# Memory attention of two token tiles written step by step in turn, in a transformer block on one core

## The chip, the cores and the metric

The kernel runs on one core of a Trainium2 chip. The core has five engines with a queue of instructions each, and every queue is worked off in order: TensorE (PE, matrix products and transposes, with its weight loads listed as PEld), VectorE (DVE), ScalarE (ACT), GpSimd (POOL) and SyncE (SP, which here only issues transfers). Matrix products land in PSUM, everything else lives in SBUF, and data comes from HBM by DMA. The metric is the device time of one execution in microseconds (us); lower is better.

## What is computed

One transformer block over 1024 tokens of width 1024, in float32: a mixer of two sparse attentions, then an attention over 256 memory rows, then a squared-ReLU MLP of width 4096. Only the middle one is touched:

```python
def _memory_xattn(h, mem, mem_norm_g, w_xq, w_xk, w_xv, xq_norm_g, xk_norm_g, w_xo):
    m = _rms_norm(mem, mem_norm_g)
    q = _rms_norm((h @ w_xq).reshape(B, L, 4, 128), xq_norm_g)
    k = _rms_norm((m @ w_xk).reshape(B, M, 4, 128), xk_norm_g)
    v = (m @ w_xv).reshape(B, M, 4, 128)
    s = jnp.einsum('bqhd,bmhd->bhqm', q, k) * (128 ** -0.5)
    p = jax.nn.softmax(s, axis=-1)
    o = jnp.einsum('bhqm,bmhd->bqhd', p, v).reshape(B, L, 512)
    return o @ w_xo

x = x + _hybrid_mixer(_rms_norm(x, norm1_g), ...)
x = x + _memory_xattn(_rms_norm(x, norm2_g), mem, ...)
x = x + _sq_relu_mlp(_rms_norm(x, norm3_g), w_ff_in, w_ff_out)
```

## The kernel before

The 1024 tokens are eight tiles of 128 rows. The work falls into two kinds. The mixer's attention (`attend`, tiles 0 to 7, eight units of output per tile, each ended by the addition at L716) has many small steps that pass from PE to DVE, ACT and POOL and back. The "fill" is the rest: projections of the second half of the tokens, the memory's keys and values (`memory`), then for tiles 0-1 and 2-3 what lies between the mixer and the MLP (`between`), the MLP of tiles 0 to 3 (`mlp`), and `between` of tiles 4-5. `together` takes turns between the two by paces written in the kernel. When the attention is done, what is left of the fill runs beside `between` of tiles 6-7 (`merge`), and the MLP of tiles 4 to 7 ends the kernel.

`between` handles two tiles: it reads the mixer's output and x, multiplies by `w_out` (L218 through `gemm`, four chunks of 256 columns; `add_to`, L899, adds the result to the residual), normalizes each tile (`norm_T2`: square and sum at L293, scale at L297, eight transposes at L274, copies out of PSUM), multiplies by `w_xq` in two chunks of 256 columns (two heads each), does the memory attention of each tile and chunk, writes the result to HBM (`xo`, L972) and reads it back (L978), transposes it, multiplies by `w_xo`, and adds it to the residual. `mlp` then normalizes its four tiles in the same way, but with the copies split in a high and a low part (ACT at L235, DVE at L236).

One item of memory attention, for one tile and one chunk, is `consume_q`, called by `gemm` as soon as the product with `w_xq` stands in PSUM. Its steps:

1. square (ACT, L934), sum (DVE, L936), gain (DVE, L937), root (DVE L229, POOL L231) and two scales (DVE L940, L941);
2. two transposes (PE, L274) and the split of the result (ACT L235, DVE L236);
3. six score products (PE), row maximum (DVE, L950, L951), two exponentials (ACT, L954);
4. four transposes (PE, L959) and their split;
5. twelve products with the values (PE), division (DVE, L971) and the write of `xo` (SP, L972).

The products with `w_out`, `w_xq` and `w_xo` are plain float32: PE takes each as two passes, two records of the trace.

PSUM is handed out in rings. In `between` of tiles 0 to 5 the ring `D` (two buffers) holds the product with `w_xq`, the scores and the products with the values, in this order; the ring `M` (one buffer) holds the transposes. Tiles 6-7 use `S` (two) and `PT` (two) instead. The SBUF ring `h` has eight buffers; keys and values of a chunk take four of them (loaded on POOL's queue at the first tile of a chunk), an item takes three.

The order in which the lines are written is not yet the order on the engines. At build a scheduler lays the instructions out for each engine, by written order and by when it reckons each one's inputs and buffers to be ready. The order that it arrives at is then fixed.

Of the kernel before, what the change touches and what calls it, by code (L numbers as in the profile page):

```python
# [166 lines left out]
def build(nc, tc, I, C, out):  # L167
# [13 lines left out]
    def pst(tag, shape):  # L181
        return psum["pool"].tile(shape, F32, tag=tag, name="ps" + tag, bufs=psum["n"][tag],
                                 padded_shape=[P, 512 // int(np.prod(shape[2:]))] + list(shape[2:]))

    def ring(pool, tag, shape, dt=F32):
        n = RINGS[pool.name if isinstance(pool.name, str) else "dn"][tag]
        return pool.tile(shape, dt, tag=tag, name=tag, bufs=n)
# [46 lines left out]
    def split_ps(src, hi, lo):  # L234
        s.activation(hi, src, AF.Copy)  # L235
        v.tensor_tensor(lo, src, hi, op=ALU.subtract)  # L236
# [31 lines left out]
    def to_T(pool, x_t, xs, nk):  # L268

        for c in range(0, nk, 4):  # L270
            m = min(4, nk - c)
            pt = pst(TAGS[pool.name][1], [P, m, P])
            for j in range(m):
                te.transpose(pt[:, j, :], x_t[:, (c + j) * P:(c + j + 1) * P], ident)  # L274
            if len(xs) == 2:
                split_ps(pt, xs[0][:, c:c + m, :], xs[1][:, c:c + m, :])
            elif c % 8 == 0:
                s.activation(xs[0][:, c:c + m, :], pt, AF.Copy)
            else:
                v.tensor_copy(xs[0][:, c:c + m, :], pt)  # L280
# [19 lines left out]
    def gemm(pool, xs, nk, nt, wsrc, chunks, consume):  # L300

        for ci, parts in enumerate(chunks):
            w = sum(n for _, n in parts)
            gr = []
            for k0 in range(0, nk, KG):
                kn = min(KG, nk - k0)
                srcs, o = [], 0
                for c0, n in parts:
                    srcs.append((lambda r, o=o, n=n: r[:, :, o:o + n],
                                 wsrc[k0 * P:(k0 + kn) * P, c0:c0 + n].rearrange("(k p) n -> p k n", p=P)))  # L310
                    o += n
                ws = load_w(pool, [P, kn, w], *srcs) if len(xs) == 2 else load_whole(pool, [P, kn, w], *srcs)
                gr += [[x[:, k, :] for x in ws] for k in range(kn)]
            for t in range(nt):
                pt = pst(TAGS[pool.name][0], [P, w])
                for k in range(nk):
                    if len(xs) == 1:
                        mm(pt, xs[0](t, k), gr[k][0], k == 0, k == nk - 1)
                        continue
                    wh, wl = gr[k]  # L320
                    xh, xl = xs[0](t, k), xs[1](t, k)
                    mm(pt, xh, wh, k == 0, False)
                    mm(pt, xh, wl, False, False)
                    mm(pt, xl, wh, False, k == nk - 1)
                consume(ci, t, pt)
                yield nk * (5 - len(xs)) * w / 2400.0
# [13 lines left out]
    def gain2(pool, src):  # L340
        gs = [ring(pool, "h", [P, 512]) for _ in range(2)]
        for i, gb in enumerate(gs):
            nc.sync.dma_start(gb, row(src[i * 512:(i + 1) * 512]).to_broadcast([P, 512]))
        return gs
# [550 lines left out]
    def residual_add(x2):  # L895
        def add_to(ci, t, pt):
            w = pt.shape[-1]
            dst = x2[t][:, ci * w:(ci + 1) * w]
            v.tensor_tensor(dst, pt, dst, op=ALU.add)  # L899
        return add_to  # L900

    def between(pool, t0, nt, x2s, keep):

        o_of = []
        for t in range(nt):
            o = ring(pool, "b4", [P, 8, P])
            for c in range(8):
                nc.sync.dma_start(o[:, c, :], oT_dr[t0 + t][c])
            o_of.append(o)
        x2 = [ring(pool, "b4", [P, DM]) for t in range(nt)]  # L910
        for t in range(nt):
            nc.sync.dma_start(x2[t], I["x"][0, (t0 + t) * P:(t0 + t + 1) * P, :])
        add_to = residual_add(x2)
        four = [[(c * 256, 256)] for c in range(4)]
        yield from gemm(pool, [lambda t, k: o_of[t][:, k, :]], 8, nt, W["w_out"], four, add_to)
        _, xf, xt_of = xT(pool, nt, True)

        gb2 = gain2(pool, W["norm2_g"])
        for t in range(nt):
            norm_T2(pool, x2[t], gb2, xt_of(t))  # L920
            yield 1.0

        kx = []

        def consume_q(ci, t, pt):
            if t == 0:
                kx[:] = [[ring(pool, "h", [P, 2, 256], F32R) for _ in range(2)] for _ in range(2)]
                for a in range(2):
                    g.dma_start(kx[0][a], KX[a][ci])
                    g.dma_start(kx[1][a], VX[a][ci])  # L930
            (kh, kl), (vh, vl) = kx
            q = ring(pool, "relu", [P, 2, 2, P])
            p3 = pt.rearrange("p (h d) -> p h d", d=P)
            s.activation(q[:, 1], p3, AF.Square)  # L934
            ss = small(pool, "xss", 2)
            v.tensor_reduce(ss, q[:, 1], axis=AX.X, op=ALU.add)  # L936
            v.tensor_tensor(q[:, 0], p3, xqg[:, None, :].to_broadcast([P, 2, P]), op=ALU.mult)  # L937
            r = rsqrt_of(pool, ss, P, 2, "xq")
            sc = small(pool, "xsc", 4).rearrange("p (a h) -> p a h", a=2)
            v.tensor_scalar(sc[:, 0, :], r, XSCALE, None, op0=ALU.mult)  # L940
            v.tensor_scalar(sc[:, 1, :], r, -XSCALE, None, op0=ALU.mult)  # L941
            qhl = ring(pool, "h", [P, 2, 2, P], F32R)
            to_T(pool, q[:, 0].rearrange("p h d -> p (h d)"), [qhl[:, 0], qhl[:, 1]], 2)
            sp = pst(TAGS[pool.name][0], [P, 2, 256])
            for h in range(2):
                mm(sp[:, h, :], qhl[:, 0, h, :], kh[:, h, :], True, False)
                mm(sp[:, h, :], qhl[:, 0, h, :], kl[:, h, :], False, False)
                mm(sp[:, h, :], qhl[:, 1, h, :], kh[:, h, :], False, True)
            nb, sums = small(pool, "xnb", 2), small(pool, "xsum", 2)
            v.tensor_reduce(nb, sp, axis=AX.X, op=ALU.max)  # L950
            v.tensor_tensor(nb, nb, sc[:, 1, :], op=ALU.mult)  # L951
            pr = ring(pool, "relu", [P, 2, 256])
            for h in range(2):
                s.activation(pr[:, h, :], sp[:, h, :], AF.Exp, bias=nb[:, h:h + 1],  # L954
                             scale=sc[:, 0, h:h + 1], accum_out=sums[:, h:h + 1])
            p2 = pst(TAGS[pool.name][1], [P, 2, 2, P])
            for k in range(2):
                for h in range(2):
                    te.transpose(p2[:, k, h, :], pr[:, h, k * P:(k + 1) * P], ident)  # L959
            ph, pl = ring(pool, "h", [P, 2, 2, P], F32R), ring(pool, "h", [P, 2, 2, P], F32R)  # L960
            split_ps(p2, ph, pl)
            pv = pst(TAGS[pool.name][0], [P, 2, P])
            for h in range(2):
                hs = slice(h * P, (h + 1) * P)
                for k in range(2):
                    mm(pv[:, h, :], ph[:, k, h, :], vh[:, k, hs], k == 0, False)
                    mm(pv[:, h, :], ph[:, k, h, :], vl[:, k, hs], False, False)
                    mm(pv[:, h, :], pl[:, k, h, :], vh[:, k, hs], False, k == 1)
            v.reciprocal(sums, sums)
            o = ring(pool, "relu", [P, 2, P])  # L970
            v.tensor_tensor(o, pv, sums[:, :, None].to_broadcast([P, 2, P]), op=ALU.mult)  # L971
            nc.sync.dma_start(xo_dr[t0 + t][:, ci * 256:(ci + 1) * 256], o.rearrange("p h d -> p (h d)"))  # L972

        yield from gemm(pool, xf, 8, nt, W["w_xq"], [[(0, 256)], [(256, 256)]], consume_q)

        for t in range(nt):
            o = ring(pool, "relu", [P, 512])
            nc.sync.dma_start(o, xo_dr[t0 + t])  # L978
            to_T(pool, o, [x[:, 0:4] for x in xt_of(t)], 4)
            yield 0.5  # L980
        yield from gemm(pool, xf, 4, nt, W["w_xo"], four, add_to)
        for t in range(nt):
            if keep:
                x2s[t0 + t] = x2[t]
            else:
                nc.sync.dma_start(x2_dr[t0 + t], x2[t])
# [151 lines left out]
```

## Time and profile before

| | us |
|---|---|
| median of 3 runs | 1861.02 |
| lowest, highest | 1859.41, 1865.53 |
| the profiled execution | 1861.12 |
| span of its trace, first to last instruction | 1859.0 |

| engine | busy us | share of the span |
|---|---|---|
| PE | 1729.4 | 93% |
| ACT | 1077.2 | 58% |
| DVE | 934.9 | 50% |
| POOL | 894.7 | 48% |

The memory attention's items start (L934) at 485.7, 500.4, 521.1 and 545.3 us for tiles 0-1, at 620.7, 636.9, 656.8 and 677.3 us for tiles 2-3, and between 1364.9 and 1439.8 us for tiles 4 to 7, where two `between` run side by side. The first eight lie beside the mixer's attention. In rows of the timeline a matmul's line begins with its start in us and its duration; `x4` counts records that follow each other; `[1.84 <-DMA whi]` is idle time before it and who ended it. A busy PE is not PE at its peak, so in what follows idle time is read together with the number of records in a stretch and with the granted clock.

### The profile page before, as it was taken

To read this page: it belongs to the slowest core of one execution; us is meant where nothing else is said; L and a number is where in the kernel's file an instruction comes from. 1 tells how busy PE (TensorE), PEld (TensorE's weight loads), DVE (VectorE), ACT (ScalarE), POOL (GpSimd) and SP (SyncE) were. 2 spreads that over 40 slices of the span, in tenths; PEclk is the share of its full clock that TensorE was granted. 3 is DMA by queue.
4 is the path that set the end of the run, shared out by engine and by line. 5 is a ranking of instruction groups with operands and counts; after the bars stand their busy time and mean duration, and the time that the engine had idled before them with its cause. 6 is when DMAs were issued, how large, how long until landed. Compare 5 with 4: busy or idle time off the path is not lost. (4 is left out here: it accounts for less than half of the span.)

```text
span 1859.0 us, 28028 instructions
## 1 busy us (share of the span) xinstructions
PE 1729.4 (93%) x9262; PEld 1467.8 (79%) x9262; DVE 934.9 (50%) x2353; ACT 1077.2 (58%) x2687; POOL 894.7 (48%) x1034
## 2 busy tenths in 40 slices
PE   5996999899989987899998999999898899999999
PEld 5995988678877776688886888888787778788787
DVE  4554766566773786466545565565333332222222
ACT  4444658898697678756984569975223233333332
POOL 2365557455451344466764766664111134444553
PEclk9998998999999998899999999999998999999999
DMA  8225413166226231121221221222773313222232
GB/s 198 71 86 163 98 35 99 65 212 178 90 86 193 88 83 42 46 70 56 77 77 57 67 72 60 64 71 93 241 249 109 116 63 97 91 91 91 91 98 101
DMA packets 180081, 187.50 MB, mean 101 GB/s; under 512 B 34657, under 2 KB 149089, under 8 KB 179937
## 3 DMA queue, kind: packets, MB, share of 16 engines
q1 hardware_dynamic: 172000, 175.23, 31.2%
q0 software_dynamic: 7936, 10.49, 2.1%
q8 instruction: 73, 1.20, 0.3%
q14 instruction: 72, 0.58, 0.1%
HBM read 164.69 MB, written 20.97 MB: 100 GB/s over the span
## 5 line engine op out<-in xcount | busy, mean ns | idle before, releaser
L249 POOL TENSOR_TENSOR wlo<-wraw,whi 128x512 fp32r<-128x512 f32 (+1 forms) x230 | 308.2, 1349 | 322.3 <-ACT whi L244 265.0
L244 ACT ACTIVATE whi<-wraw 128x512 fp32r<-128x512 f32 (+2 forms) x289 | 180.9, 628 | 251.8 <-PE psS L218 150.0
L218 PE MATMUL psD<-whi,xh 128*128 128x256 f32 (+1 forms) x704 | 192.7, 357 | 5.8 <-ACT whi L244 3.5
L218 PE MATMUL psD<-wlo,xh 128*128 128x256 f32 (+1 forms) x704 | 192.5, 354 | 0.8 <-DMA wlo<-in_w_in_dram 0.6
L218 PE MATMUL psD<-whi,h 128*128 128x512 f32 x512 | 177.1, 406 | 9.4 <-POOL h L1024 3.7
L236 DVE TENSOR_TENSOR pl<-psPT,ph 128x512 fp32r<-128x512 f32 (+1 forms) x232 | 141.8, 620 | 62.2 <-ACT ph L235 61.2
L218 PE MATMUL psS<-whi,h 128*128 128x512 f32 x512 | 162.0, 392 | 5.1 <-DVE b L899 5.1
L688 ACT ACTIVATE S<-S,mn 128x128 f32<-128x128 f32 (+7 forms) x192 | 142.8, 745 | 38.9 <-DVE mn L686 38.2
L235 ACT ACTIVATE ph<-psPT 128x512 fp32r<-128x512 f32 (+1 forms) x232 | 122.9, 541 | 57.7 <-PE psPT L703 50.0
L249 DVE TENSOR_TENSOR wlo<-wraw,whi 128x512 fp32r<-128x512 f32 (+1 forms) x59 | 59.4, 1007 | 175.5 <-ACT whi L244 171.8
L218 PEld LDWEIGHTS psD<-whi,xh 128*128 128x128 f32 x704 | 132.7, 195 | 17.2 <-ACT whi L244 3.9
L218 PEld LDWEIGHTS psD<-wlo,xh 128*128 128x128 f32 x704 | 133.6, 195 | 12.7 <-DMA wlo<-in_w_in_dram 1.0
L703 PE MATMUL psPT<-c_ident,S 128*128 128x128 f32 x816 | 133.9, 279 | 10.3 <-POOL S L693 4.7
L693 POOL TENSOR_SCALAR S<-S,sums,gi 128x640 f32<-128x640 f32 (+7 forms) x128 | 107.4, 850 | 68.2 <-DVE sums L691 59.2
L899 DVE TENSOR_TENSOR b<-psS,b 128x512 f32<-128x512 f32 (+1 forms) x80 | 50.0, 636 | 140.9 <-PE psS L218 140.8
L218 PEld LDWEIGHTS psD<-whi,h 128*128 128x128 f32 x512 | 95.8, 190 | 31.6 <-POOL h L1024 5.0
L218 PEld LDWEIGHTS psS<-whi,h 128*128 128x128 f32 x512 | 96.0, 188 | 29.4 <-DVE b L899 9.4
L218 PE MATMUL psS<-K,qh 128*128 128x384 f32 (+3 forms) x288 | 109.2, 383 | 6.6 <-DVE mn L686 2.6
L703 PEld LDWEIGHTS psPT<-c_ident,S 128*128 128x128 f32 x816 | 97.0, 142 | 20.8 <-POOL S L693 8.1
L899 DVE TENSOR_TENSOR b<-psD,b 128x512 f32<-128x512 f32 (+1 forms) x112 | 63.2, 572 | 87.6 <-PE psD L218 76.0
L218 PE MATMUL psD<-xh,wlo 128*128 128x512 f32 x256 | 102.1, 401 | 0.7 <-POOL wlo L249 0.7
L218 PE MATMUL psD<-wlo,h 128*128 128x512 f32 x256 | 102.3, 402 | 0.0
(299 smaller groups left out, 4643.7 us busy)
## 6 DMA issues: line engine op xcount, KB each, us to landing
wraw<-in_w_ff_in_dram SPq DMA_DIRECT2D x128, 256.0 KB, 2.8
wraw<-in_w_ff_out_dram SPq DMA_DIRECT2D x128, 256.0 KB, 2.7
whi<-in_w_out_dram SPq DMA_DIRECT2D x32, 256.0 KB, 5.3
wlo<-in_w_out_dram SPq DMA_DIRECT2D x32, 256.0 KB, 5.2
wraw<-in_w_in_dram SPq DMA_DIRECT2D x24, 256.0 KB, 3.7
q<-st SPq DMA_DIRECT2D x12, 512.0 KB, 2.6
qin<-q SPq DMA_DIRECT2D x44, 128.0 KB, 2.3
x<-in_x_dram SPq DMA_DIRECT2D x8, 512.0 KB, 5.2
```

The source lines that it names most:

```text
L218: te.matmul(o, a, b, start=start, stop=stop)
L235: s.activation(hi, src, AF.Copy)
L236: v.tensor_tensor(lo, src, hi, op=ALU.subtract)
L244: s.activation(hi, raw, AF.Copy)
L249: (v if l == "v" else g).tensor_tensor(lo, raw, hi, op=ALU.subtract)
L688: s.activation(S, S, AF.Exp, bias=low, scale=-1.0, accum_out=sums[:, hh:hh + 1])
L693: g.tensor_scalar(Ss[hh], Ss[hh], sums[:, hh:hh + 1], 1.0 if gate is None else gate[:, hh:hh + 1], op0=ALU.mult, op1=ALU.mult)
L703: te.transpose(p2[:, j, hh, :], S[:, (c + j) * P:(c + j + 1) * P], ident)
L899: v.tensor_tensor(dst, pt, dst, op=ALU.add)
```

## The change

`consume_q` no longer does an item at once. It keeps the product of the first tile of a pair (`pts`) and returns; at the second tile it makes a generator for each of the two items and advances them in turn, so that the written order is step 1 of both, step 2 of both, and so on. The generator yields at four places, between the five steps listed above. No instruction is added, removed or resized; the rings are the same.

```diff
-        kx = []
+        kx, pts = [], {}
 
         def consume_q(ci, t, pt):
             if t == 0:
@@
                     g.dma_start(kx[0][a], KX[a][ci])
                     g.dma_start(kx[1][a], VX[a][ci])
+            pts[t] = pt
+            if t % 2 == 0 and t + 1 < nt:
+                return
+            both = [(u, pts.pop(u)) for u in sorted(pts)]
+            steps = [memory_item(ci, u, x) for u, x in both]
+            while steps:
+                steps = [x for x in steps if next(x, None) is not None]
+
+        def memory_item(ci, t, pt):
+
             (kh, kl), (vh, vl) = kx
...
             v.tensor_scalar(sc[:, 1, :], r, -XSCALE, None, op0=ALU.mult)
+            yield 1
             qhl = ring(pool, "h", [P, 2, 2, P], F32R)
             to_T(pool, q[:, 0].rearrange("p h d -> p (h d)"), [qhl[:, 0], qhl[:, 1]], 2)
+            yield 1
             sp = pst(TAGS[pool.name][0], [P, 2, 256])
...
                              scale=sc[:, 0, h:h + 1], accum_out=sums[:, h:h + 1])
+            yield 1
             p2 = pst(TAGS[pool.name][1], [P, 2, 2, P])
...
             split_ps(p2, ph, pl)
+            yield 1
             pv = pst(TAGS[pool.name][0], [P, 2, P])
```

## The prediction

> **What bounds the kernel.** I read the page first, then the chain of waits, then the windows by stage, and last the waits and the timeline of the two stages that stood out.
>
> ```profile
> span 1859.0 us, 28028 instructions
> PE   5996999899989987899998999999898899999999
> PEclk9998998999999998899999999999998999999999
> ```
>
> PE is at 9 tenths in most slices; the dips lie in the attention (slices 7 to 17) and in slices 29 to 32, where attention ends and the MLP of tiles 4 to 7 hasn't begun.
>
> ```profile
> 1522.99 44.12 PE psS L218 x191
> 485.00:560.00 75.00, 68.85 (x438) 57.00 (x437) 60.12 (x177) 63.38 (x173) 38.45 (x58) 1.00 0.27 81
> 615.00:700.00 85.00, 77.56 (x497) 66.01 (x496) 70.39 (x216) 61.18 (x161) 39.31 (x57) 1.00 0.24 69
> 722.00:756.00 34.00, 20.46 (x78) 15.57 (x77) 19.66 (x39) 29.15 (x70) 10.35 (x14) 0.60 0.05 14
> 756.00:1301.00 545.00, 532.95 (x2783) 447.51 (x2782) 307.92 (x705) 382.33 (x841) 347.43 (x342) 0.99 0.22 69
> 1380.00:1465.00 85.00, 75.47 (x393) 62.66 (x392) 30.74 (x94) 24.72 (x65) 11.01 (x17) 0.92 0.37 113
> 1493.00:1859.00 366.00, 357.14 (x1537) 288.43 (x1536) 86.41 (x107) 113.95 (x187) 170.97 (x145) 0.99 0.29 92
> ```
>
> The first line is of the chain: the last MLP runs 191 PE records of 512 columns in 44.12 us, 0.23 each, with nothing between. The others are windows: length, then busy us and count for PE, PEld, DVE, ACT, POOL, then granted clock. From 756 to 1301 and from 1493 on PE is the bound, and order is worth nothing there. Time is lost in three places. The memory attention of tiles 0-1 and 2-3 (485 to 560, 615 to 700) leaves PE idle for 75.00 - 68.85 = 6.2 and 85.00 - 77.56 = 7.4 us. From 722 to 756, where the MLP of tiles 0 to 3 begins with its four norms, 34 us hold only 78 PE records: even at 0.23 each that is 17.9, so 16 us are lost, at a clock of 0.60. The tail (1380 to 1465), where the last eight items run, idles 9.5 us at a clock of 0.92, which is 85 x 0.08 = 6.8 us more.
>
> **What the change moves.** No instruction is new, so the whole effect is the order at each engine. I compared the two built orders. On PE they agree up to the first item and again from the last MLP's first block; between them the fill moves ahead of the attention. From the first score product to the last value product of tiles 0-1, 261 attention instructions stood in between, and 156 do now; for tiles 2-3, 266 and 100. So the MLP of tiles 0 to 3 begins when 35 to 37 units of attention are done, where it was 40 or 41, and `w_out` of tiles 4-5 is nearly through when the attention ends, where it had begun. The attention that is displaced ends up beside the MLP or that `w_out`.
>
> **Term 1, the norms of the first MLP.** The transposes have one PSUM buffer, `M`, and each group of four waits until DVE has read the last:
>
> ```profile
> PE psM L274 <- DVE xl L236: 7.5, 4, 2.0
> 739.11 1.08 PE L274 MATMUL psM<-c_ident,relu 128*128 128x128 f32 x4 [1.98 <-DVE xl L236]
> 742.08 1.09 PE L274 MATMUL psM<-c_ident,relu 128*128 128x128 f32 x4 [1.89 <-DVE xl L236]
> 749.80 0.80 PE L218 MATMUL psD<-xh,whi 128*128 128x512 f32 x1 [0.81 <-ACT xh L235]
> 1305.98 0.28 PE L218 MATMUL psPV<-ph,Vd 128*128 128x256 f32 x1
> 1306.10 0.28 PE L218 MATMUL psPV<-pl,Vd 128*128 128x256 f32 x1
> 1440.63 1.28 PE L218 MATMUL psS<-h 128*128 128x128 f32 x10
> ```
>
> A group takes 742.08 - 739.11 = 3.0 us, eight groups 24, whatever stands between. In the old order 20 attention instructions stood among the eight groups; now 100 do, 10 to 22 between each two. A product follows the one before it after 0.12 us when PE doesn't wait (the last rows: 1306.10 - 1305.98, and ten in under 1.28), so the stage takes up 80 x 0.12 = 9.6 us of work that PE does elsewhere today. Those instructions also load ACT and DVE, which the groups pass through; I charge each group 0.5 us, nearly one split copy, 4 us in all. With PE less idle the MLP needn't start at half clock: from 749.8 to the stretch's end at 756 it ran slowly, worth half of 6.2, 3 us. Sum -9.6 + 4 - 3 = about -9; bounds 0 (the groups stretch by all they take in) and -16 (the whole loss of the row). I take the middle since 13 instructions between groups are about 1.6 us of the 3.0.
>
> **Term 2, items beside attention.** The idle 6.2 + 7.4 = 13.6 us belong mostly to the attention's own waits. Fewer attention instructions pass through these stretches, and the two items now fill each other's waits; against that, the waits of a pair follow each other more closely on PE, whose queue is held up as a whole by one late transpose. I take -3; bounds -8 (over half of the idle time) and +6 (as much again in one stretch). POOL's loads of keys and values wait as before for the value products of the chunk before, and are first needed after two products with `w_xq` where it was one: no cost. SP's writes of `xo` leave in pairs; what follows them in SP's queue are weights loaded ahead.
>
> **Term 3, the end of the attention.** Its last units ran beside the MLP, whose products are always ready; now they run beside `w_out`, norms and the first pair of tiles 4-5. Window 756 to 1301 idles 12 us in 545; I charge +2 for a stretch like one of term 2 cut to a third; bounds 0 and +5.
>
> **Term 4, the tail.** Today two streams go in step there, each item in turn with one of the other stream, so a pair in turn is already on show:
>
> ```profile
> 1425.58 0.38 PE L274 MATMUL psM<-c_ident,relu 128*128 128x128 f32 x2
> 1429.98 0.33 PE L959 MATMUL psM<-c_ident,relu 128*128 128x128 f32 x1 [0.80 <-ACT relu L954]
> 1433.25 0.69 DVE L236 TENSOR_TENSOR h<-psPT,h 128x512 fp32r<-128x512 f32 x1 [0.47 <-ACT h L235]
> 1390.68 0.42 DVE L971 TENSOR_TENSOR relu<-psD,xsum 128x256 f32<-128x256 f32 x1 [4.98 <-PE psD L218]
> xo<-relu SPq DMA_DIRECT2D x16, 128.0 KB, 1.9
> relu<-xo SPq DMA_DIRECT2D x8, 256.0 KB, 2.9
> PE psM L959 <- ACT relu L954: 4.1, 7, 1.6
> 1328.39 0.28 PE L218 MATMUL psPV<-pl,Vd 128*128 128x256 f32 x1
> 1337.14 1.03 PE L218 MATMUL psD<-whi,b 128*128 128x256 f32 x4
> 1338.01 1.03 PE L218 MATMUL psD<-wlo,b 128*128 128x256 f32 x4
> 1346.05 1.96 PE L218 MATMUL psS<-whi,b 128*128 128x256 f32 x8 [1.84 <-DMA whi<-in_w_out_dram]
> ```
>
> In the new order the streams fall out of step: tiles 4-5 are a chunk ahead. Three of the four pairs have products with `w_out` or `w_xo` of the other stream between their steps. Of the 9.5 + 6.8 = 16.3 us lost today I take three quarters as gone: -12. But the last pair of tiles 6-7 stands alone: after its second product with `w_xq` come 4 transposes, 12 score products, 8 transposes and 24 value products in one piece, then the transposes of `xo`. From first transpose to last split such a pair takes 1433.25 + 0.69 - 1425.58 = 8.4 us; then 12 value products (1.3), the division (0.4), the write (1.9) and the read (2.9): 14.9 us, about a us less for the first tile, then 4 transposes and a copy, so `w_xo` starts some 15 us after the product. PE has 48 instructions, 5.3 us, to do in it: +9.7, and a quarter of the 6.8 us of clock for a start at half rate, +1.7. At the tail's beginning the first `w_out` product of tiles 6-7 comes 1346.05 - 1328.67 = 17.4 us after the last value product of the attention, since outputs, x and weights load one behind the other. Today `w_out` of tiles 4-5 fills all but 1.84. In the new order there are 36 short instructions (4.0 us), some 1.5 us of a pair's waits and 16 products with `w_xq` at (1338.01 - 1337.14) / 2 = 0.43 (6.9): PE idles 5 rather than 1.8, and 1.5 in the pair: +4.5. Sum -12 + 9.7 + 1.7 + 4.5 = +4; bounds -6 (the cover also takes the last pair's copies) and +16 (nothing of the 16.3 is regained).
>
> **Sum.** -9 - 3 + 2 + 4 = -6 on the profiled execution's 1861.1 us (its span is 1859.0), which stands 0.1 above the median of the runs shown: 1855, and for the median the same. A measurement here tells about 0.3%, 5.6 us, from no change.
>
> **Rivals.** *The norms stay slow* (chance 0.15): the eight groups stretch as far as the attention placed among them, since ACT is busy 29.15 of 34 us in that stretch and DVE 19.66. Term 1 is 0, the rest -3 + 2 + 4: 1864. For it speaks that each group needs one ACT and one DVE copy behind attention copies of the same length; against it that ACT's 29.15 are partly the next tile's index search, which is placed elsewhere now.
>
> *The pairs take all of PSUM* (chance 0.26), the slower one: a pair holds both buffers of `D` (or `S`) with its two products from step 1 to the scores, then with the scores, then with the values, so its stream's next product with `w_xq` can't run inside it. Today one tile's product (8 x 0.43 = 3.4 us) runs inside each item pair of the tail. It decides where the other stream has less than 3.4 us ready per pair. If that is so in all four pairs, 13.8 us come on top of what I expect less the 1.7 of clock: -6 + 12 = +6, 1867. Against it stand the passes of `w_out` and `w_xo` in the built order, which are plain products with their weights loaded ahead. Beside this: the Trainium skill, Perfetto Trace Analysis, section Optimization Strategy, reads the same gap repeated on the engine that should be full as a sign that SBUF or PSUM is too short for the next tile. By that rule the change, which holds two tiles at once in a ring of two, would go the wrong way, to the 1867 of this mechanism; no run so far shows which.
>
> *Everything gained* (chance 0.16): term 1 at -16 and term 2 at -8, the rest as above: 1843.
>
> My forecast keeps 0.43, its own range 1848 to 1860. Of that 0.27 lies beyond 5.6 us of gain and 0.16 within; with the third rival faster is 0.43. The first rival adds 0.10 to no change and 0.05 to slower: 0.26, and 0.31 with the second. The range is 1843 to 1870: it reaches past the second rival and down to the third.
>
> **What would show it.** Right: the eight norm groups of the MLP between about 640 and 710 us with attention between them and a clock near 1; the items of a pair within 1 to 3 us of each other; the attention's last unit some 10 to 20 us later than at 1329; a hole of some 10 us before the last `w_xo`, followed by a lower clock; one of 5 us before the first `w_out` of tiles 6-7. Wrong: holes in PE before every pair's transposes in the tail, norm groups 4 us or more apart, or new idle time inside the long MLP stretch, which I have taken as full on both sides.

## The result and the profile after

The changed kernel takes 1835.78 us (median of four runs, 1832.64 to 1836.17) against 1861.45 for the kernel before on the same chip: a ratio of 0.9856, 95% interval 0.9836 to 0.9876. That is 25.7 us less where 6 were forecast, and below the range. The profiled execution took 1835.75 us, its span is 1833.9.

The page of the changed kernel, its busy tenths and the granted clock in 40 slices:

```profile
span 1833.9 us, 28049 instructions
...
PE   5996999889989998999999999999999799999999
...
PEclk9997998999999999999999999999989799999999
```

PE, its weight loads, DVE, ACT and POOL run 9262, 9262, 2353, 2687 and 1034 instructions in both kernels; the 21 that the page counts more are not among them. Seven slices are below 9 tenths of PE, where eleven were. The 7 that is left, slice 32 at a clock of 7 tenths, holds the end of the tail and the norms behind it.

The windows of the changed kernel, cut at the same events as those of the kernel before further down (columns as in the prediction: length, busy us and count of PE, PEld, DVE, ACT, POOL, then clock, DMA share, GB/s):

```profile
489.00:545.00 56.00, 52.19 (x339) 44.67 (x338) 44.97 (x132) 41.40 (x114) 30.48 (x44) 1.00 0.29 83
...
616.70:660.50 43.80, 41.86 (x258) 35.08 (x259) 33.41 (x116) 26.70 (x74) 17.43 (x25) 1.00 0.30 91
...
691.80:726.60 34.80, 28.98 (x172) 23.87 (x172) 30.84 (x86) 33.22 (x87) 14.53 (x22) 0.95 0.05 15
726.60:1250.00 523.40, 515.77 (x2676) 431.47 (x2675) 294.02 (x667) 391.66 (x885) 346.90 (x345) 0.99 0.22 70
1250.00:1330.20 80.20, 77.73 (x458) 69.00 (x457) 49.12 (x122) 36.97 (x71) 17.66 (x20) 0.98 0.47 150
...
1330.20:1455.80 125.60, 115.07 (x564) 99.31 (x563) 38.04 (x107) 28.47 (x71) 15.64 (x23) 0.89 0.57 177
```

The kernel before, cut in the same way (first item to last division of tiles 0-1; the same for tiles 2-3; third square of the MLP's norms (L293) to 6 us behind the MLP's first product; last unit of the attention to the norms of the last MLP):

```profile
485.70:560.20 74.50, 68.35 (x436) 56.46 (x434) 60.23 (x177) 63.53 (x174) 38.65 (x58) 1.00 0.28 82
620.70:694.10 73.40, 67.64 (x441) 57.75 (x440) 62.32 (x195) 53.86 (x145) 33.30 (x47) 1.00 0.23 66
...
726.60:755.80 29.20, 17.59 (x63) 13.60 (x62) 15.88 (x31) 24.35 (x59) 7.62 (x11) 0.53 0.03 7
...
1329.10:1479.10 150.00, 138.53 (x695) 117.58 (x693) 46.93 (x132) 34.46 (x83) 18.11 (x27) 0.95 0.56 174
```

A pair of tiles now passes its memory attention in 56.0 and 43.8 us rather than 74.5 and 73.4, with 339 and 258 PE records rather than 436 and 441 in it: the mixer's attention that stood there has gone elsewhere. So a shorter window alone is no gain; the work in it has to be taken off. I counted the PE records of each window by kind and gave each the distance at which its kind follows itself in the trace when PE doesn't wait (0.11 us a transpose; 0.113, 0.118 and 0.174 a product of 128, 256 and 384 columns; 0.216 a pass of a plain float32 product; 0.230 a product of 512 columns). The window less this work is called lost time here: waits, half clock and gaps between records together.

| stage, lost us of its length | before | after | difference |
|---|---|---|---|
| items of tiles 0-1 | 15.3 of 74.5 | 8.8 of 56.0 | -6.5 |
| from there to the items of tiles 2-3 | 7.0 of 60.5 | 10.3 of 71.7 | +3.3 |
| items of tiles 2-3 | 15.2 of 73.4 | 7.7 of 43.8 | -7.5 |
| `w_xo` up to the norms | 6.4 of 32.5 | 2.8 of 31.3 | -3.6 |
| norms of the first MLP | 21.0 of 29.2 | 11.9 of 34.8 | -9.1 |
| first MLP, to 1250 us | 26.9 of 494.2 | 23.3 of 523.4 | -3.6 |
| end of the attention | 6.7 of 79.1 | 6.3 of 80.2 | -0.4 |
| tail | 25.2 of 150.0 | 26.0 of 125.6 | +0.8 |
| norms of the last MLP | 10.2 of 13.7 | 9.3 of 13.0 | -0.9 |
| sum | 133.9 | 106.4 | -27.5 |

Before the first item stand 485.7 and 489.0 us of work that the change doesn't touch (+3.3), and the last MLP took 366.2 and 365.1 (-1.1). The sum, -27.5 + 3.3 - 1.1 = -25.3, is the difference of the spans, 1859.0 - 1833.9 = 25.1, within rounding. So this table says where the time went: 14.3 us in the four stretches from the first item to the norms, 9.1 in the norms, 3.6 in the first MLP, and nothing in the tail.

### The profile page after: what moved, and what is told of

Its sections match the earlier page's. It is cut to its first block, busy times and chain, and to the rows that moved or that the text cites. A ratio compares the mean times of both kernels' runs of the same rounds, so it can differ in the third digit from the quotient of the medians.

```text
span 1833.9 us, 28049 instructions
## 1 busy us (share of the span) xinstructions
PE 1726.9 (94%) x9262; PEld 1474.2 (80%) x9262; DVE 936.1 (51%) x2353; ACT 1074.6 (59%) x2687; POOL 895.0 (49%) x1034
## 5 line engine op out<-in xcount | busy, mean ns | idle before, releaser
L249 DVE TENSOR_TENSOR wlo<-wraw,whi 128x512 fp32r<-128x512 f32 (+1 forms) x59 | 64.3, 1090 | 166.9 <-ACT whi L244 166.8
L218 PEld LDWEIGHTS psD<-whi,xh 128*128 128x128 f32 x704 | 134.0, 198 | 14.3 <-ACT whi L244 3.3
L218 PEld LDWEIGHTS psS<-whi,h 128*128 128x128 f32 x512 | 96.1, 188 | 29.3 <-DVE b L899 9.3
L218 PE MATMUL psS<-K,qh 128*128 128x384 f32 (+3 forms) x288 | 113.5, 397 | 5.6 <-DVE mn L686 2.8
L899 DVE TENSOR_TENSOR b<-psD,b 128x512 f32<-128x512 f32 (+1 forms) x112 | 63.2, 572 | 74.5 <-PE psD L218 73.0
```

The source lines that it names most:

```text
L218: te.matmul(o, a, b, start=start, stop=stop)
L249: (v if l == "v" else g).tensor_tensor(lo, raw, hi, op=ALU.subtract)
```

## The experiments

An expectation names the theories that it weighs. By letter: theory A, with its variants, holds that the turns themselves save the time, by covering the waits of a pair, and so shortening what hangs on it. Theory C holds that much of the 25 us is the alignment of one fixed order on the engines, which any other edit would also shift. A rival B is told where it stands, and A2 is theory A as it was put after the first four runs. Ratios are to the kernel before, measured beside each group of runs. The lost times that the readings use, and the lead, the time from the first square of tiles 4-5 to the first of tiles 6-7:

| kernel | ratio to before | items 0-1 to norms | norms | first MLP and end of attention | tail | lead |
|---|---|---|---|---|---|---|
| before | 1 | 43.9 | 21.0 | 33.6 | 25.2 | 26.5 |
| after | 0.9856 | 29.6 | 11.9 | 29.6 | 26.0 | 66.9 |
| e1_hold | 0.9940 | 44.5 | 13.9 | 27.2 | 28.4 | 42.0 |
| e2_turn03 | 0.9975 | 28.9 | 11.9 | 32.5 | 47.2 | 70.6 |
| e3_turn47 | 0.9953 | 43.2 | 19.5 | 36.1 | 17.6 | 27.7 |
| e4_turn23 | 1.0025 | 35.9 | 10.6 | 36.8 | 44.1 | 64.3 |
| e5_turn01 | 0.9995 | 38.2 | 15.6 | 31.9 | 34.9 | 53.8 |
| e6_rev | 0.9976 | 40.7 | 13.2 | 39.6 | 26.8 | 64.6 |
| e7_normD | 0.9956 | 42.8 | 12.8 | 27.5 | 30.6 | 46.2 |
| e8_rest30 | 0.9858 | 28.8 | 11.9 | 30.7 | 25.4 | 67.5 |
| e9_normD_after | 0.9958 | 28.3 | 8.7 | 41.8 | 35.0 | 88.9 |
| y_two | 0.9874 | 32.0 | 11.0 | 31.7 | 22.6 | 65.8 |
| y_one | 0.9981 | 40.2 | 10.2 | 39.4 | 30.5 | 60.5 |
| y_first | 0.9922 | 46.0 | 19.0 | 31.0 | 14.4 | 31.0 |
| z_mix | 0.9941 | 29.3 | 12.9 | 31.1 | 43.2 | 71.7 |
| z_hold67 | 0.9938 | 29.0 | 11.9 | 30.9 | 37.4 | 66.9 |
| z_hold45 | 0.9887 | 29.1 | 11.9 | 34.0 | 28.1 | 71.3 |

The four columns of lost time in a row, added and set against those of the kernel before, give its measured time to about 4 us in every row.

I call the tail's two streams in step where the lead is 26 to 31 us, as in the kernel before, and out of step where it is above 53. The tail's loss goes with it. Without turns in the tail it is 25.2, 28.4, 30.6, 34.9, 44.1 and 47.2 us at leads of 26.5, 42.0, 46.2, 53.8, 64.3 and 70.6 (before, e1_hold, e7_normD, e5_turn01, e4_turn23, e2_turn03). With all turns it is 17.6 at 27.7, 25.4 to 26.8 at 64.6 to 67.5, and 35.0 at 88.9.

**The product held, the items one behind the other.** Against the changed kernel:

```diff
             both = [(u, pts.pop(u)) for u in sorted(pts)]
-            steps = [memory_item(ci, u, x) for u, x in both]
-            while steps:
-                steps = [x for x in steps if next(x, None) is not None]
+            for u, x in both:
+                drain(memory_item(ci, u, x))
```

> The first tile's product is held until the second's, as in the change, but the two items are then written one behind the other, not in turn. Theory A (the steps in turn fill each other's waits, so that the memory attention of tiles 0 to 3 needs less attention beside it and the fill gets ahead): holding alone gives nothing, 1856 to 1868 us, and the items of tiles 2-3 spread over some 75 us from first square to last division, as before (620.7 to 694.1). Theory B (the gain comes from having both products first): about 1836. Theory C (any new order of the scheduler's would have given such a difference): any value, with no relation to the length of the items' stretch.

Measured: 1852.31 us (1848.36 to 1854.09), ratio 0.994 (0.992 to 0.9961). That is far from theory B's 1836, but below the 1856 to 1868 that theory A gave for it. Keeping the first product until the second stands is worth some 9 us without any turn, though not where the turns save: the four stretches lose 44.5 us, as before (43.9). The gain lies in the norms (13.9 for 21.0) and in the MLP behind them. The turns add the other 16.

**Turns for some pairs only.** Each kernel differs from the changed one in a condition; e3_turn47 has `t0 >= 4`, e4_turn23 `t0 == 2`, e5_turn01 `t0 == 0` in place of `t0 < 4`. The tiles that don't meet it neither take turns nor keep a product, as in the kernel before:

```diff
+            if not (t0 < 4):
+                drain(memory_item(ci, t, pt))
+                return
             pts[t] = pt
```

> In turn for tiles 0 to 3 alone, beside the attention; tiles 4 to 7 as before. Theory A: nearly the whole gain, 1833 to 1842 us, since the tail lost 25 us of PE time before and after the change. If the gain is in the tail: about 1861. Theory C: no relation to the parts.

Measured: 1857.33 us, ratio 0.9975 (0.9965 to 0.9985). Theory A had 1833 to 1842. Up to the first item of tiles 4-5 it is the changed kernel. Its tail gives nearly all of it back: 47.2 us lost. The windows and some PE rows of that tail:

```profile
1328.70:1479.20 150.50, 130.75 (x582) 108.24 (x580) 39.79 (x112) 28.73 (x68) 16.25 (x24) 0.84 0.48 154
```

```profile
1434.96 1.19 PE L218 MATMUL psS<-h 128*128 128x256 f32 x6 [0.47 <-ACT h L235]
1437.88 0.33 PE L975 MATMUL psPT<-c_ident,relu 128*128 128x128 f32 x1 [1.72 <-ACT relu L969]
...
1448.75 0.41 PE L274 MATMUL psPT<-c_ident,relu 128*128 128x128 f32 x2 [1.27 <-DVE xqms L229]
1449.64 1.27 PE L218 MATMUL psS<-h 128*128 128x256 f32 x6 [0.47 <-ACT h L235]
1452.66 1.45 PE L975 MATMUL psPT<-c_ident,relu 128*128 128x128 f32 x4 [1.75 <-ACT relu L969]
1454.79 3.12 PE L218 MATMUL psS<-h 128*128 128x128 f32 x12 [0.69 <-ACT h L235]
```

Tiles 4-5 are through, and the last two items of tiles 6-7 stand alone, one behind the other. Each step waits for the copy or the exponentials ahead of it (0.47, 1.72; then 1.27, 0.47, 1.75, 0.69), twice over, and the clock falls: twelve products take 3.12 us here and 1.64 in the tail of the kernel before, where other products stand ahead of them. By the granted clock alone this tail is short of up to 150.5 x 0.16 = 24 us of PE time, that of the changed kernel of 125.6 x 0.11 = 14.

> In turn for tiles 4 to 7 alone, in the tail; tiles 0 to 3 as before. Theory A: 1857 to 1866 us, the tail's cover of three pairs paid back by the last pair that stands alone and by the wait for w_out of tiles 6-7. If the gain is in the tail: 1836 to 1845. Up to the first item of tiles 4-5 the trace must be that of the kernel before, with the norms of the first MLP at 723 to 728 us.

Measured: 1854.44 us, ratio 0.9953 (0.9934 to 0.9972), a little below theory A's 1857 to 1866 and far from the 1836 to 1845 of a gain in the tail. Turns in the tail alone, with the streams in step as before, lose 17.6 us there for 25.2. So the turns are worth 7.6 us in a tail in step, and 47.2 - 26.0 = 21 in one out of step.

> In turn for tiles 2-3 alone. Theory A: these tiles' stretch went from 85 to 45 us and lost 10 us of PE time less, and the norms of the first MLP follow it directly, so most of the gain is here: 1838 to 1848 us, with the norms at about 690 us and attention between their transposes. If the lead has to come from both pairs: 1848 to 1856, half of the gain. Theory C: no relation.

Measured: 1866.63 us, ratio 1.0025 (1.001 to 1.004): slower than before, with turns in one of the four pairs of tiles, where theory A had 1838 to 1848, or 1848 to 1856. Tiles 2-3 do shorten (45.6 us for 73.4), the norms lose 10.6, and the tail, now out of step and without turns, 44.1.

> In turn for tiles 0-1 alone, the six others one item behind the other as before. The counterpart in tiles 2-3 alone measured 1866.6 and in tiles 0 to 3 1857.3, both with the tail's two streams out of step (47 and 44 us lost there). Theory A: tiles 0-1 lose 8 to 10 us rather than 15.3, tiles 2-3 lose some 14, and the fill is ahead by less; if the tail stays in step 1850 to 1856, if it falls out of step 1860 to 1868. Theory C: the first stretch loses between 8 and 16 whatever is done, 1855 to 1868.

Measured: 1860.96 us, ratio 0.9995 (0.9983 to 1.0008). Tiles 0-1 lose 8.8 us as theory A has it, tiles 2-3 16.9; the tail, out of step at a lead of 53.8, loses 34.9. The time lies at the lower end of what theory A gave for that, and within theory C's range too, so it decides nothing; tiles 0-1 run in the same order as in the changed kernel here. The parts aren't additive: tiles 0-1 alone +0, tiles 2-3 alone +5, tiles 4 to 7 alone -8, all of them -26 us.

**The mirror image.** The second tile of a pair goes first at each step:

```diff
-            both = [(u, pts.pop(u)) for u in sorted(pts)]
+            both = [(u, pts.pop(u)) for u in sorted(pts, reverse=True)]
```

> The change with the two items of a pair taken in turn the other way round, second tile first. After the first four runs two things are left: theory A2 (turns shorten the items' stretches beside the attention, the fill gets ahead of it, and the tail, whose streams are then out of step, needs the turns too, so that the parts don't add up) and theory C (the scheduler's order is so sensitive that 25 us can come from any edit). A2: 1830 to 1842 us, with stretches of the items, norms and tail as in the changed kernel to within 5 us of lost time each. C: anywhere between 1835 and 1866.

Measured: 1856.34 us (1852.63 to 1860.91), ratio 0.9976 (0.9962 to 0.9991), 20.6 us above its mirror image; theory A2 had 1830 to 1842. Tiles 2-3 (45.5 us long, 9.4 lost), the norms (13.2) and the tail (26.8) are nearly those of the changed kernel. What is lost again is lost elsewhere: 15.0 us at tiles 0-1, where 8.8 were, and 39.6 for 29.6 in the first MLP and at the end of the attention, half of it in each. The window of tiles 0-1 shows where the first comes from:

```profile
492.20:550.00 57.80, 53.35 (x313) 46.36 (x311) 46.06 (x134) 42.74 (x119) 30.58 (x45) 0.88 0.27 78
```

The clock is 0.88 there and 1.00 in the changed kernel (57.8 x 0.12 = 6.9 us). It was 0.5 from 504 to 514 us, and why it fell there isn't shown. At the end of the attention PE waits for weights, at the head of the waits from 1250 to 1348.6 us:

```profile
PE psD L218 <- DMA whi<-in_w_out_dram: 3.4, 1, 3.4
```

So theory C holds for a part: two orders with the same turns lie 20 us apart, 6 of it by the clock at tiles 0-1 and 10 behind the norms.

**Fewer handovers.** y_two keeps the handovers behind the scales and behind the exponentials, y_first the former alone, y_one the latter alone (each drops lines `yield 1`). Here theory A foretold a length of tiles 2-3 and a time for each, theory C only a time.

> The change with two handovers of four: the items of a pair change over only behind the scales (step 1) and behind the exponentials (step 3); the transposes of q go with the scores, the split of p with the value products. Theory A (the turns themselves hide the copies that a pair waits for; two handovers lie on the two longest of these waits, behind the norm and behind the exponentials): within 0.4% of the change, 1834 to 1843, with tiles 2-3 in 43 to 48 us and the tail's loss within 5 us of 26. Theory C (much of the 25 us is the alignment of one particular order): some 8 to 20 us given back, 1844 to 1856, with no stage of its own that loses it.

Measured: 1836.65 us (1835.81 to 1839.92), ratio 0.9874 (0.9861 to 0.9887). Two handovers do what four do, as theory A has it; tiles 2-3 take 46.6 us.

> The change with one handover, behind the exponentials (step 3). Theory A: each item runs steps 1 to 3 whole, so the waits for its norm and for the split of q lie open again, and only the wait for the exponentials is covered: 1843 to 1852, tiles 2-3 in 50 to 62 us. Theory C: anything from 1835 to 1860, and the stretch of tiles 2-3 does not tell which.

Measured: 1858.0 us, ratio 0.9981 (0.9969 to 0.9993), above theory A's 1843 to 1852 and within theory C's range.

> The change with one handover, behind the scales (step 1): the two norms side by side, then the items one behind the other. Theory A: the norm is the longest chain of an item without PE, so this keeps more than the handover behind the exponentials, 1840 to 1850, tiles 2-3 in 48 to 60 us. Theory C: as for the other, 1835 to 1860.

Measured: 1847.07 us (1843.4 to 1849.22), ratio 0.9922 (0.9909 to 0.9935). The windows of tiles 2-3 in y_one:

```profile
624.30:682.70 58.40, 54.09 (x359) 47.40 (x358) 47.73 (x150) 37.67 (x97) 27.32 (x38) 1.00 0.27 82
```

and in y_first, with its tail below:

```profile
621.30:690.60 69.30, 62.91 (x390) 52.68 (x388) 53.20 (x170) 45.00 (x117) 29.76 (x43) 0.98 0.20 62
1333.70:1467.70 134.00, 127.78 (x670) 110.57 (x668) 46.09 (x130) 34.09 (x83) 18.12 (x27) 0.97 0.59 189
```

The length of a pair goes by the handovers: 73.4 us with none, 69.3 with the one behind the norm, 58.4 with the one behind the exponentials, 46.6 with both, 43.8 with four. So the exponentials are the longer wait, against theory A as I had put it (69.3 where 48 to 60 was expected). The lost time says it more sharply: tiles 0-1 and 2-3 together lose 30 us with no handover, 32 with the one behind the norm, 23 with the one behind the exponentials, 19 with both and 16 with four. In these stretches the handover behind the norm pays only beside the other. The total doesn't follow this length: y_one has the shorter pairs and is 11 us slower than y_first, whose tail, in step, lost only 14.4; y_one's, at a lead of 60.5, lost 30.5.

**The tail taken apart.** z_mix keeps all handovers for tiles 0 to 3 and only the one behind the scales for the others; z_hold67 takes the turns from tiles 6-7 alone, z_hold45 from tiles 4-5 alone. The edit of z_hold67 (z_hold45 has `t0 == 4`; z_mix puts `if t0 < 4:` ahead of the last three lines `yield 1`):

```diff
+            if t0 == 6:
+                for _ in memory_item(ci, t, pt):
+                    pass
+                return
             pts[t] = pt
```

> Tiles 0 to 3 with all four handovers as in the change; tiles 4 to 7 with the one behind the scales alone. With that one handover everywhere the tail lost 14 us, with all four 26. Theory A (the handover does it: two norms side by side, then products in long pieces): the tail loses 14 to 20, 1824 to 1832. Rival B (the 14 came from the lesser lead of the fill, by which the two streams of the tail stayed in step): with the lead of the change the tail loses 26 to 40, 1836 to 1850.

Measured: 1850.51 us (1847.97 to 1853.58), ratio 0.9941 (0.9929 to 0.9954); the tail loses 43.2, both a little above what rival B gave. That decides against theory A: with the same handover in the tail y_first lost 14.4 us at a lead of 31.0, and z_mix 43.2 at 71.7. Both waits for the exponentials (`psM` and `psPT`; 0.4 and 1.1 us in the changed kernel) are open again in the waits of that tail:

```profile
PE psM L974 <- ACT relu L967: 4.5, 7, 1.8
PE psPT L974 <- ACT relu L967: 3.5, 2, 1.8
PE psS L218 <- DMA whi<-in_w_out_dram: 3.0, 1, 3.0
```

> In turn for tiles 0 to 5; tiles 6-7 one item behind the other. Without turns in tiles 4 to 7 the tail lost 47 us, with them 26. Theory A (what the turns save is in the pairs that stand alone at the end, tiles 6-7): the tail loses 40 to 47, 1849 to 1857. Rival B (either pair covers the other stream's waits, so each is worth half): 33 to 39, 1842 to 1848.

Measured: 1849.88 us (1846.47 to 1854.23), ratio 0.9938 (0.9924 to 0.9951); its tail loses 37.4. The time is that of theory A, the loss that of rival B (the profiled execution was one of the shorter ones, with a span of 1844.7).

> The counterpart: in turn for tiles 0 to 3 and 6-7; tiles 4-5 one item behind the other. Theory A: the tail loses 26 to 31, 1835 to 1841. Rival B: 33 to 39, 1842 to 1848.

Measured: 1838.89 us, ratio 0.9887 (0.9871 to 0.9902); its tail loses 28.1. With neither pair in turn the tail loses 47.2, with tiles 4-5 37.4, with tiles 6-7 28.1, with both 26.0. Turns in the pair of tiles that ends alone are worth 19 us by themselves, in the other pair 10 by themselves but 2 beside them. Theory A is the nearer: of its four ranges only the loss of z_hold67 (40 to 47) was missed.

**The norms by themselves.** The transposes of the first MLP's norms go to ring `D` (two buffers) rather than `M` (one); once in the kernel before, once in the changed one (`norm_T2` and `to_T` hand the ring on, which is left out here). The same line serves the last MLP, whose norms go from `PT` to `S`, both of two buffers; they lose 10.1 us in either kernel, for 10.2 and 9.3:

```diff
-            norm_T2(pool, x2[t], gb3, xt_of(t))
+            norm_T2(pool, x2[t], gb3, xt_of(t), TAGS[pool.name][0])
```

> The kernel before, with the transposes of the four norms of the first MLP in ring D (two buffers, idle there) instead of M (one): one suspected wait taken away, nothing written in turn. If the one buffer makes the 21 us that PE loses there: the stage from the first norm's transposes to the MLP shortens from 23 to about 14 us, 1849 to 1855 us in all if the rest stays. If the missing attention makes it: the stage stays at 20 us or more, no change.

Measured: 1854.29 us, ratio 0.9956 (0.9941 to 0.997). The norms lose 12.8 us for 21.0, at a clock that stays higher (0.76 from 720 to 756 us, where the kernel before had 0.62). Transposes of that stage in its timeline:

```profile
729.08 1.97 PE L274 MATMUL psD<-c_ident,relu 128*128 128x128 f32 x8 [0.88 <-DVE relu L297]
...
734.67 1.91 PE L274 MATMUL psD<-c_ident,relu 128*128 128x128 f32 x8
```

Of the eight groups the first four go through two at a time. The single buffer made some 8 of the 21 us, as was expected (1849 to 1855), and the change gets as much out of the stage (11.9) by putting attention into the gaps.

> Both: the changed kernel with the norms' transposes in ring D. The norm stage gets shorter (12 us lost to 6), but the fill gets still further ahead, and both pairs of tiles 6-7 then stand alone in the tail. A2: the tail loses 10 us more than the changed kernel's 26, the norms 6 less: 1836 to 1844 us. If the lead alone makes the gain: below 1832.

Measured: 1854.0 us, ratio 0.9958 (0.9944 to 0.9971), well above both theories. On top of the change the second buffer gains 3.2 us more in the norms (8.7 for 11.9) and loses 12 in the first MLP and at the end of the attention, which neither theory had, and 9 in the tail, where both pairs of items of tiles 6-7 now stand alone. A local gain that puts the fill further ahead costs at the end.

**A pace of the tail.** `REST`, the weight of what is left of the fill beside tiles 6-7, is 30 rather than 70:

> The changed kernel with the pace of the remaining fill in the tail lowered (REST 70 to 30), so that passes with w_xo of tiles 4-5 are kept for the last pair of tiles 6-7, which stands alone in the changed kernel. If what the tail still loses (26 us) is the last pair standing alone: about 8 us of it go, 1825 to 1831 us. If it is the wait for w_out and the clock: 1832 to 1838.

Measured: 1835.35 us, ratio 0.9858 (0.9843 to 0.9873): the changed kernel again, with 25.4 us lost in the tail. The passes of tiles 4-5 do stand among the steps of the last pair now, and that pair up to `w_xo` loses 8.5 us for 11.4, but the stretch ahead of it loses as much more. No kernel of the study beats the changed one.

## Why the prediction was wrong in size

The direction was right, -25.7 us was not -6. The step that failed is Term 2, "items beside attention": -3, bounds -8 and +6. Its two stretches, tiles 0-1 and 2-3, measured -14.0, and with what lies between and up to the norms -14.3. Of the 19 us that the forecast was short, this is 11.3; the first MLP, put at nothing, is 3.6, Term 4 3.2 and Term 3 2.4; the start of the trace took 3.3 back and its end gave 2.0. Two things were wrong in Term 2.

First its base. I took what could be gained from PE's idle time, 6.2 + 7.4 us. Cut at the items' own events the windows idle 74.50 - 68.35 = 6.2 and 73.40 - 67.64 = 5.8 us, but lose 15.3 and 15.2. A record that waits for the next is shown with its whole duration, 0.28 us, where one that is followed at once takes up 0.12; so a queue of short, broken pieces looks fuller than it is. The weight loads tell it better: 74.50 - 56.46 = 18.0 and 73.40 - 57.75 = 15.7 us without one, and after the change 56.00 - 44.67 = 11.3 and 43.80 - 35.08 = 8.7. These differences, 6.7 and 6.9, are nearly those of the lost time, 6.5 and 7.5. The Trainium skill, Perfetto Trace Analysis, section Identifying the Most-Contended Engine, says that matmul busy time is no good measure of how near TensorE is to its limit, because pipelined instructions look smaller in the trace, and to go by the arithmetic done against the peak and by the share of weight loads. This case agrees in these two stretches that busy time misleads, though the error went the other way here: broken pieces look larger. In the last MLP, where PE is full, the weight loads are busy only 288.97 of 366 us, so the measure serves for stretches of short products.

Second, what a pair costs. I thought of the items as filling the attention's waits and the reverse, and so of a balance near zero. In truth a pair is a chain of waits, and its length went from 73.4 to 43.8 us as handovers were added (y_first, y_one, y_two), most of the lost time going with the one behind the exponentials; the attention that was displaced ran later beside the MLP, whose stage took 523.4 us for 494.2 and yet lost 3.6 us less. I had taken that stretch as full on both sides and so at zero, though it is not a gain to count on: e6_rev, with the same turns, doesn't have it.

The other terms came out near, two of them partly by luck:

- Term 1, the norms: -9 forecast, -9.1 measured. The mechanism was right, but the agreement in size is luck. The forecast had 9.6 us of work taken up, 4 of stretch and 3 saved by the clock; the stage took up 14.7 us (22.9 for 8.2 by the spacing of its records) and got 5.6 longer (34.8 for 29.2), clock included. The groups of four in the changed kernel's timeline:

```profile
694.08 0.60 PE L274 MATMUL psM<-c_ident,relu 128*128 128x128 f32 x4
...
699.43 1.06 PE L274 MATMUL psM<-c_ident,relu 128*128 128x128 f32 x4
...
702.23 0.60 PE L274 MATMUL psM<-c_ident,relu 128*128 128x128 f32 x4
...
714.15 0.63 PE L274 MATMUL psM<-c_ident,relu 128*128 128x128 f32 x4 [0.79 <-DVE xl L236]
```

  They hardly wait for the buffer any more, since attention stands between them, as the waits of that stage say:

```profile
PE psM L274 <- DVE xl L236: 1.0, 2, 0.8
```

  The clock is 0.95 where it was 0.53. The groups are 2.8 to 5.4 us apart, though; the sign that I had named for being wrong, 4 us or more, came for three of the seven distances and meant nothing, because PE mostly worked in between. They lie at 694 to 722 us, not between 640 and 710.
- The items of a pair: the first steps of both lie 4.3 us apart (ACT, L944, at 616.74 and 621.04 us), rather than 1 to 3, since the second product with `w_xq` ends that much later.
- Term 3, the end of the attention: +2 forecast, -0.4 measured, just outside its bounds of 0 and +5. Its last unit came at 1330.2 us, 1 us later than before and not 10 to 20: at the end of tile 4 it was 30 us behind (740.0 for 709.6, by the additions that end a unit), and by 1330 it had made that up beside the MLP.
- Term 4, the tail: +4 forecast, +0.8 measured, and its parts separately: the beginning up to the first `w_out` of tiles 6-7 lost 8.6 us for 2.0 (forecast +4.5), the middle 2.2 for 22.7 (forecast -12), the last pair up to `w_xo` 11.4 (forecast 9.7 + 1.7), and `w_xo` behind it 3.6 for 0.5 (not in the forecast). So the sum is near because the middle gained 8 us more than I had taken, and the beginning and `w_xo` lost 5 more. The beginning in the changed kernel's timeline:

```profile
1333.49 0.69 PE L218 MATMUL psD<-h 128*128 128x128 f32 x2 [1.51 <-ACT h L235]
...
1334.99 4.94 PE L218 MATMUL psD<-h 128*128 128x128 f32 x22
...
1349.51 0.67 PE L218 MATMUL psS<-whi,b 128*128 128x256 f32 x2 [0.67 <-DMA whi<-in_w_out_dram]
```

  The wait for `w_out` is 0.67 us, not the 5 that I looked for; the loss is the pair's own wait and the half clock behind it (22 products in 4.94 us; granted clock 0.61 from 1331.5 to 1341 us). The last pair in windows and timeline:

```profile
1420.50:1438.03 17.53, 11.72 (x54) 9.28 (x52) 5.79 (x17) 5.02 (x14) 1.98 (x2) 0.65 0.40 129
```

```profile
1420.52 0.38 PE L274 MATMUL psPT<-c_ident,relu 128*128 128x128 f32 x2
1421.48 0.50 PE L218 MATMUL psS<-h 128*128 128x256 f32 x2 [0.58 <-ACT h L235]
...
1425.00 0.33 PE L972 MATMUL psPT<-c_ident,relu 128*128 128x128 f32 x1 [0.84 <-ACT relu L966]
...
1428.29 4.96 PE L218 MATMUL psS<-h 128*128 128x128 f32 x22 [0.42 <-ACT h L235]
1436.25 1.09 PE L274 MATMUL psPT<-c_ident,relu 128*128 128x128 f32 x4 [3.01 <-DMA relu<-xo]
```

  The hole stands where it was forecast, 3.0 us of it the way of `xo` to HBM and back; most of the rest is half clock: 22 products in 4.96 us.

The first rival, norms that stay slow, is out: Term 1 would have been 0. The second, pairs that take all of PSUM, is out in the form in which I gave it: the middle of the tail lost 2.2 us where it should have lost 13.8 more than forecast. The rule of the Trainium skill named there (Perfetto Trace Analysis, section Optimization Strategy) is that the same gap repeated can mean too little SBUF or PSUM. It held in another place: for the norms, where a second buffer took the loss from 21.0 to 12.8 us (e7_normD). The third rival, 1843, came nearest and was still 7 us short, and that near by luck: it had Term 1 at -16, 7 us too much, and Term 2 at -8, 6 too little.

What stays open: how much of the 25.7 us would outlast another edit. Tiles 2-3, the norms and a tail with turns keep their gain in both mirror images; the 10 us in the first MLP and at the end of the attention and the 6 at tiles 0-1 don't. By which instruction the first of these orders falls better was not traced further.

## What to carry to other kernels

Where short products wait on each other, count PE's records by kind and take their work from the stretch, or read the weight loads; idle time of PE understates what there is to gain, here 6 us for 15. Writing two independent items in turn pays by its handovers behind the longest waits (two of four did all of it), and it moves everything behind: turns in one pair of tiles of four cost 5 us, because the two streams at the end fell out of step (a lead of 64 us for 26) without turns there. So judge such a change by all stages, and measure it in its parts and in its mirror image before saying what it is worth.

## What was not expected of the hardware

The changed kernel, e2_turn03, z_mix, z_hold67 and z_hold45 are written alike up to tiles 4-5. Their items of tiles 0-1 and 2-3 take 56.0 to 56.2 and 43.8 to 43.9 us in all five traces. But the first item starts at 489.0, 488.9, 484.7, 487.1 and 484.1 us: a spread of 5 us ahead of any instruction that differs (in all kernels of this study PE, ACT, DVE and POOL run the same instructions in the same order up to that item), while from there to the attention's last unit they take 839.8 to 842.8. Over this study the start lay between 483.6 and 492.2 us, a spread larger than the whole effect that I had forecast. What makes it isn't shown. Comparing stages rather than spans takes this out.

The clock came back late. Behind the thin stretch above (granted clock 0.65) the first passes of `w_xo` in the changed kernel's timeline are these:

```profile
1438.03 2.07 PE L218 MATMUL psS<-whi,xh 128*128 128x256 f32 x4 [0.69 <-ACT xh L278]
1439.89 1.91 PE L218 MATMUL psS<-wlo,xh 128*128 128x256 f32 x4
...
1446.91 1.03 PE L218 MATMUL psS<-whi,xh 128*128 128x256 f32 x4
1447.77 1.03 PE L218 MATMUL psS<-wlo,xh 128*128 128x256 f32 x4
```

Four passes take 1439.89 - 1438.03 = 1.86 us at first, and 1447.77 - 1446.91 = 0.86 later on; the granted clock is 0.53 from 1438 to 1443 us and 1.00 from 1443 to 1448. So a pause of the pair goes on costing after PE has work again, 3.1 us more in this `w_xo`.
